# The first mixer of a two-layer hybrid decoder: four conv tiles by Silu, the q products of both token tiles together, and three sets of order edges for the state-space decays

## The chip, the cores and the metric

The kernel runs on one core of a Trainium2 chip. The metric is device microseconds of one execution of the whole program. Before the change the median of three runs is 1026.51 us (1025.82 to 1027.15).

The engines are named as in the profile: PE is TensorE (PEld its weight loads), DVE is VectorE, ACT is ScalarE, POOL is GpSimd, SP is SyncE.

## The reference, cut to what matters

Two layers. Each is a feed-forward block, a mixer and a feed-forward block, all added to the residual x (256 tokens by 1024, float32). The change touches only the mixer of the first layer, which joins a state-space part (SSD, 16 heads in 4 groups) and a latent attention part (MLA, 8 heads):

```python
xbc = silu(causal_depthwise_conv(h @ w_xbc, w, b))   # 2048 columns: x | B | C
dt  = softplus(dt_raw + bias);  a = dt * A           # A = -exp(a_log)
a_cs = cumsum(a)                                     # within a chunk of 128 tokens
CB   = C @ B.T                                       # per chunk and group
Lmat = exp(a_cs[l] - a_cs[s]) for s <= l, else 0     # "decays", per head
y_diag = (CB * Lmat) @ (x * dt)
y_off  = exp(a_cs) * (C @ state)
y = rms_norm((y_diag + y_off + d_skip * x) * silu(z))
q = rms_norm(q_a @ w_qb); k, v = from(kv_a @ w_kvb)  # rope on 32 of 96 columns
o = softmax(q @ k.T, causal) @ v
x = x + concat(y, o) @ w_out
```

The outputs must agree with this to float32-like accuracy, which is why each product is made of three.

## The kernel before, in words

**Weights.** Every weight matrix is loaded once, in pieces of at most 128 x 1024 float32 (512 KB), in the order in which the program uses them. `Stream.load` issues the load on SP's queue into `raw` (four buffers, L89), ACT casts it to `wh` (L93, eight buffers, float32r) and DVE writes what the cast lost into `wl` (L96, eight buffers). This DVE subtraction is called the *split* below. A `raw` buffer is free for the next load when its split is done. A product is three matmuls: hi x hi, hi x lo and lo x hi (L298 to L300 for products by token, L315 to L317 by channel, L345 to L347 for the output projection).

**Tokens and banks.** The 256 tokens are two tiles of 128, t = 0 and 1. PSUM has four banks for products (`bank`, names `p_...`), and two plus two for small ones (`sbank`, names `m_...`). A product that takes a bank waits for the last reader of the product that held it.

**The order of the work.** The program is written in one order, and a scheduler with a timeline simulation then lays out the instruction order of each engine. It may move an instruction past others that are ready later by its estimate. `self.order(later, earlier)` adds an edge to it: in the laid out order `later` may not stand ahead of `earlier`. On the chip every engine works through its own list in order, and waits on semaphores where an operand or a buffer comes from another engine.

**The first mixer** (some 196 to 376 us of the profiled execution) is written so:

1. `xbc(8)` to `xbc(11)`: the four column tiles of B. `xbc(c, out)` loads one tile of weights, makes the product with 24 matmuls of 256 columns, and `conv_silu` makes the convolution: one ACT instruction (L489) and three of DVE (L491). Silu is then made of `Tanh` on ACT (L494) and one more DVE instruction (L495).
2. The q products `p_qb`, for t = 0 and then t = 1: two halves each, of nine matmuls of 384 columns. ACT reads each half three times (square L575, and the copies `qnat` L577 and `qr` L578). After the two halves of a tile come its rope, its norm factor, its eight transposes `m_qT` and the copies of them (L588).
3. `xbc(12)`, the kv products `p_kvb` of t = 0, `xbc(13)`, those of t = 1. ACT reads each p_kvb three times (square L606, `V` L608, `knat` L609); the transposes `m_kT` are copied with a gain to `kT` (L620).
4. softplus and the decay sums: `dte` by Abs and Exp (L421, L424; the Exp needs a table load), a polynomial on DVE (L428), `dts` L626, `a` L630, the cumulative sum `m_acs` on PE (L633), its transpose, and a write to DRAM by POOL (`acs_rows`, L642). Each row is later read back, spread over all partitions.
5. `xbc(14)` and `xbc(15)`, then the scores and softmax of both tiles and the products with V (`m_att_o`).
6. `decays(t)`: `m_CB` (L694), its masked copy `cb` (L696, DVE), two loads `E` (L700, POOL's queue, 512 KB each), sixteen Relu (L706) and four Exp (L709) on ACT, and four products with cb on DVE (L712). Only the first Relu of a tile is ordered behind the softmax.
7. `xbc(0)` to `xbc(7)` and their transposes `m_xsT`, then `scan(0)` (`m_yd`, L746), `decays(1)`, and the four products `p_z` with their gates (ACT Tanh L758, DVE L759). `p_z` holds all four product banks, so the first matmul of the output projection `p_acc` takes the bank that the first gate has read.
8. The norm of the gated y, the states, `scan(1)`, and the output projection `p_acc`.

The lines that the change touches are L88 to L97, L418 to L432, L484 to L495, L549 to L588, L624 to L647, L687 to L716 and L748.

Of the kernel before, what the change touches and what calls it, by code (L numbers as in the profile page):

```python
# [7 lines left out]
F32 = dt.float32  # L8
# [3 lines left out]
AF = mybir.ActivationFunctionType  # L12
ALU = mybir.AluOpType
X = mybir.AxisListType.X

P = 128
# [34 lines left out]
ROW = {}  # L51
# [21 lines left out]
class Stream:  # L73
# [4 lines left out]
    def __init__(self, nc, pool, flat, raw_bufs, bufs):  # L78
        self.nc, self.pool, self.flat = nc, pool, flat
        self.raw_bufs, self.bufs = raw_bufs, bufs  # L80
        self.off = 0
        self.n = 0

    def load(self, widths):
        nc = self.nc
        res = []
        for i, x in enumerate(widths):
            raw = self.pool.tile([P, x], F32, tag="raw", name=f"raw{self.n}_{i}", bufs=self.raw_bufs)  # L88
            nc.sync.dma_start(out=raw, in_=self.flat[self.off:self.off + P * x].rearrange("(p w) -> p w", w=x))  # L89
            self.off += P * x  # L90
            hi = self.pool.tile([P, x], F32R, tag="wh", name=f"wh{self.n}_{i}", bufs=self.bufs)
            lo = self.pool.tile([P, x], F32R, tag="wl", name=f"wl{self.n}_{i}", bufs=self.bufs)
            self.cast = nc.scalar.copy(out=hi, in_=raw)  # L93
            if i == 0:
                self.first = self.cast
            nc.vector.tensor_tensor(out=lo, in0=raw, in1=hi.bitcast(F32), op=ALU.subtract)  # L96
            res.append((hi, lo))  # L97
        self.n += 1
        return res


class Net:
# [380 lines left out]

    def conv_silu(self, c, b, out):  # L484

        nc = self.nc
        cw = self.conv[:, c, :]
        v = self.small([P, S], "cv", bufs=3)
        nc.scalar.activation(out=v, in_=b, func=AF.Identity, scale=cw[:, 3:4], bias=cw[:, 4:5])  # L489
        for s in (1, 2, 3):  # L490
            nc.vector.scalar_tensor_tensor(out=v[:, s:], in0=b[:, :S - s], scalar=cw[:, 3 - s:4 - s], in1=v[:, s:],  # L491
                                           op0=ALU.mult, op1=ALU.add)
        th = self.small([P, S], "cth", bufs=2)
        self.tanh = nc.scalar.activation(out=th, in_=v, func=AF.Tanh)  # L494
        return nc.vector.scalar_tensor_tensor(out=out, in0=th, scalar=1.0, in1=v, op0=ALU.add, op1=ALU.mult)  # L495
# [12 lines left out]
    def mixer0(self, hT, x, after):  # L508
# [39 lines left out]

        def xbc(c, out):  # L549
            w = st.load([D])[0]  # L550
            b = self.bank([P, S], "xbc")
            self.in_ch(b, hT, w)
            return self.conv_silu(c, b, out)
        for i in range(4):
# [7 lines left out]
        kT = [self.blk([96, 8, P], f"kT{t}", grp="a") for t in range(2)]  # L562
        sq = self.small([P, 2, 8], "sqs")
        for t in range(2):
            qn = self.blk([P, 8, 96], "qnat", grp="a")
            qr = self.blk([P, 8, 2, 16], "qr")
            for j in range(2):
# [9 lines left out]
                nc.scalar.copy(out=qn[:, hs, :64], in_=b[:, :, :64])  # L577
                nc.scalar.copy(out=qr[:, hs, :, :], in_=b[:, :, 64:].rearrange("p a (s d) -> p a s d", s=2))  # L578
            roped = self.apply_rope(qn[:, :, 64:].rearrange("p a (s d) -> p a s d", s=2), qr, t, "q", 8)

# [10 lines left out]
        for t in range(2):  # L591
# [24 lines left out]
            for j in range(2):  # L616
                tp = self.tbank([96, 4, P], "kT", "a")
                for i in range(4):
# [4 lines left out]
        e = self.small([P, 2, 16], "dte")  # L623
        l1 = self.log1p_exp(dtv, e, "dtl", squares)  # L624
        dts = self.edge.tile([P, 2, 16], F32, tag="dts", name="dts", bufs=1)
        nc.vector.scalar_tensor_tensor(out=dts, in0=dtv, scalar=0.0, in1=l1, op0=ALU.max, op1=ALU.add)  # L626
        ea = self.small([P, 16], "ea")
        nc.scalar.activation(out=ea, in_=row[:, ROW["a_log"]], func=AF.Exp)
        a = self.small([P, 32], "a")
        nc.vector.scalar_tensor_tensor(out=a.rearrange("p (t h) -> p t h", t=2), in0=dts, scalar=-1.0,  # L630
                                       in1=ea.unsqueeze(1).broadcast_to([P, 2, 16]), op0=ALU.mult, op1=ALU.mult)
# [14 lines left out]
        for i in (2, 3):  # L646
            xbc(12 + i, BC[1][:, i, :])  # L647

# [31 lines left out]
        exps = []  # L680
# [9 lines left out]
        def decays(t):  # L690
# [7 lines left out]
            for j in range(2):  # L698
                h = 16 * t + 8 * j
                nc.gpsimd.dma_start(out=E[j], in_=rows[h:h + 8, :].partition_broadcast(P))  # L700
            for g in range(4):
                eb = E[g // 2][:, 4 * (g % 2):4 * (g % 2) + 4, :]

                for i in range(4):
                    h = t * 16 + 4 * g + i
                    first = nc.scalar.activation(out=eb[:, i, :], in_=eb[:, i, :], func=AF.Relu, scale=-1.0, bias=acs[:, h:h + 1])  # L706
                    if g == i == 0:
                        self.order(first, exps[t])
                nc.scalar.activation(out=eb, in_=eb, func=AF.Exp, scale=-1.0)  # L709
# [4 lines left out]

        E0 = decays(0)

# [23 lines left out]
        def scan(t, E):  # L740
            for j in range(2):
# [5 lines left out]
                nc.vector.tensor_tensor(out=xs[t][:, s], in0=b.rearrange("p a b -> p (a b)"), in1=xs[t][:, s], op=ALU.add)  # L747
        scan(0, E0)  # L748
        E1 = decays(1)

# [482 lines left out]
```

## Time and profile before

| | before |
|---|---|
| median of three runs | 1026.51 us (1025.82 to 1027.15) |
| the profiled execution | 1026.63 us, its span 1024.9 us |
| PE busy | 1004.7 us (98%) |
| DVE, ACT, POOL busy | 680.5, 573.9, 72.1 us |
| granted PE clock | 0.9 or more of full speed in each of 40 slices |
| DMA | 181 GB/s mean over the span |

The span is that of the trace, from the first to the last instruction; the 1.7 us beside it belong to the execution but not to the trace. Matmuls are pipelined: a record of a 128 x 512 matmul lasts about 0.39 us though the next one starts 0.23 us after it. So the time between two starts is what a matmul costs in a row of them, and a wait of PE costs the idle time that the trace shows and a little more, since the pipeline runs empty ahead of it.

### The profile page before, as it was taken

What the parts mean: (1) busy time and instruction counts of PE and PEld (TensorE: products, weight loads), DVE (VectorE), ACT (ScalarE), POOL (GpSimd) and SP (SyncE); (2) the same over time, 40 slices, a digit from 0 to 9 for tenths busy, and PEclk for the clock granted to TensorE, in tenths of its full rate; (3) what the DMA queues carried; (4) which work ended last, traced back from release to release, by engine and by line L of the source; (5) the groups of instructions that cost most, each with busy time, mean ns of one, the idle gap of its engine ahead of it and who ended that gap; (6) DMA issues with size and microseconds to landing.
All of it is one profiled execution on the core that took longest, in us unless ns stands there. A gap on an engine that the chain in (4) does not pass through costs nothing.

```text
span 1024.9 us, 15128 instructions
## 1 busy us (share of the span) xinstructions
PE 1004.7 (98%) x5609; PEld 863.5 (84%) x5609; DVE 680.5 (66%) x1053; ACT 573.9 (56%) x1043; POOL 72.1 (7%) x108
## 2 busy tenths in 40 slices
PE   6999999999999999999999999999999999999998
PEld 5888888898988888888888888888887778888886
DVE  6787754588796767677546767754578676776641
ACT  5665543388866466655434665553386456555530
POOL 2100000016132200000000000000020000000000
PEclk9999999999999999999999999999999999999999
DMA  8775555455455257555564655555564256555451
GB/s 294 265 224 190 196 181 185 137 204 173 146 171 174 87 196 255 188 195 193 187 198 150 229 192 194 187 183 169 165 209 140 84 164 199 192 185 188 162 185 42
DMA packets 52090, 185.95 MB, mean 181 GB/s; under 512 B 5911, under 2 KB 5928, under 8 KB 52016
## 3 DMA queue, kind: packets, MB, share of 16 engines
q1 hardware_dynamic: 49248, 176.58, 52.0%
q0 software_dynamic: 2048, 6.83, 2.1%
q10 hardware_dynamic: 720, 1.57, 0.4%
q8 instruction: 44, 0.72, 0.3%
q14 instruction: 30, 0.25, 0.1%
HBM read 183.89 MB, written 1.06 MB: 180 GB/s over the span
## 4 chain that ended last, share of the span: by engine, by line
PE 93%; ACT 3%; DMA 2%; DVE 1%; issue 1%; POOL 1%; POOLq 0%; DVEq 0%; ACTq 0%
PE p_u L326 13%; PE p_g L326 13%; PE p_acc L346 9%; PE p_acc L345 9%; PE p_acc L347 9%; PE p_u L328 7%; PE p_g L328 7%; PE p_u L300 1%; PE p_u L298 1%; PE p_u L299 1%; PE p_g L298 1%; PE p_g L299 1%; PE p_g L300 1%; PE m_nrm L135 1%; PE p_xbc L315 1%; PE p_tok L298 1%
## 5 line engine op out<-in xcount | busy, mean ns | idle before, releaser
L96 DVE TENSOR_TENSOR wl<-raw,wh 128x1024 fp32r<-128x1024 f32 (+3 forms) x341 | 410.2, 1213 | 222.5 <-ACT wh L93 220.8
L93 ACT CAST wh<-raw 128x1024 fp32r<-128x1024 f32 (+3 forms) x341 | 352.3, 1040 | 298.3 <-PE p_acc L346 99.5
L326 PE MATMUL p_g<-hT,wh 128*128 128x512 f32 x576 | 203.2, 391 | 0.0
L326 PE MATMUL p_u<-hT,wh 128*128 128x512 f32 x576 | 203.1, 391 | 0.0
L328 PE MATMUL p_g<-hT,wl 128*128 128x256 f32 x576 | 161.6, 281 | 0.0
L328 PE MATMUL p_u<-hT,wl 128*128 128x256 f32 x576 | 161.3, 280 | 0.0
L347 PE MATMUL p_acc<-wl,acth 128*128 128x512 f32 x352 | 137.1, 389 | 0.0
L346 PE MATMUL p_acc<-wh,actl 128*128 128x512 f32 x352 | 137.0, 389 | 0.0
L345 PE MATMUL p_acc<-wh,acth 128*128 128x512 f32 x352 | 136.2, 391 | 0.0
L326 PEld LDWEIGHTS p_u<-hT,wh 128*128 128x128 f32 x576 | 107.7, 187 | 23.8
L326 PEld LDWEIGHTS p_g<-hT,wh 128*128 128x128 f32 x576 | 107.8, 187 | 23.6
L328 PEld LDWEIGHTS p_g<-hT,wl 128*128 128x128 f32 x576 | 108.8, 189 | 0.2
L328 PEld LDWEIGHTS p_u<-hT,wl 128*128 128x128 f32 x576 | 108.9, 189 | 0.0
L347 PEld LDWEIGHTS p_acc<-wl,acth 128*128 128x128 f32 x352 | 66.1, 188 | 13.8
L345 PEld LDWEIGHTS p_acc<-wh,acth 128*128 128x128 f32 x352 | 66.1, 188 | 13.6
L346 PEld LDWEIGHTS p_acc<-wh,actl 128*128 128x128 f32 x352 | 66.1, 188 | 13.4
L255 POOL TENSOR_TENSOR ss<-ss,mhalf 128x1 f32<-128x1 f32 x12 | 6.7, 558 | 578.7 <-DVE ss L273 578.7
L353 DVE SCALAR_TENSOR_TENSOR x<-p_acc,x 128x512 f32<-128x512 f32 x24 | 16.4, 688 | 39.4 <-PE p_acc L347 39.4
L315 PE MATMUL p_xbc<-hT,wh 128*128 128x256 f32 x128 | 36.8, 288 | 0.9 <-DVE cv L491 0.9
L317 PE MATMUL p_xbc<-hT,wl 128*128 128x256 f32 x128 | 36.6, 286 | 0.0
L316 PE MATMUL p_xbc<-hT,wh 128*128 128x256 f32 x128 | 36.2, 283 | 0.0
L409 DVE TENSOR_TENSOR sg<-sg 128x256 f32<-128x256 f32 x72 | 30.6, 425 | 7.8 <-DVE sg L406 0.9
(373 smaller groups left out, 1495.5 us busy)
## 6 DMA issues: line engine op xcount, KB each, us to landing
raw<-in_w SPq DMA_DIRECT2D x326, 512.0 KB, 4.3
gain<-in_gains POOLq DMA_DIRECT2D x5, 512.0 KB, 5.6
E<-acs_rows POOLq DMA_DIRECT2D x4, 512.0 KB, 6.1
raw<-in_w SPq DMA_DIRECT2D x4, 400.0 KB, 3.1
raw<-in_w SPq DMA_DIRECT2D x4, 288.0 KB, 2.8
raw<-in_w SPq DMA_DIRECT2D x3, 384.0 KB, 3.5
raw<-in_w SPq DMA_DIRECT2D x4, 272.0 KB, 2.9
out<-x ACTq DMA_DIRECT2D x4, 256.0 KB, 2.0
```

Source lines behind the costliest of these rows:

```text
L93: self.cast = nc.scalar.copy(out=hi, in_=raw)
L96: nc.vector.tensor_tensor(out=lo, in0=raw, in1=hi.bitcast(F32), op=ALU.subtract)
L298: mm(out, ah, wh, start=first and i == 0, stop=False)
L315: mm(out, hi[:, cs], xh, start=k == 0, stop=False)
L316: mm(out, hi[:, cs], xl, start=False, stop=False)
L317: mm(out, lo[:, cs], xh, start=False, stop=k == KT - 1)
L326: first = mm(out, hi[:, cs], hT[k // 2][:, k % 2], start=k == 0, stop=k == KT - 1, skip_group_check=True)
L328: second = mm(out[:, 0, :], lo[:, cs], self.hk(hT, k)[0], start=False, stop=k == KT - 1, skip_group_check=True)
L345: first = nc.tensor.matmul(o, ah, w[0][:, s], start=k == 0, stop=False)
L346: nc.tensor.matmul(o, al, w[0][:, s], start=False, stop=False)
L347: nc.tensor.matmul(o, ah, w[1][:, s], start=False, stop=k == nk - 1)
L409: nc.vector.tensor_tensor(out=sg, in0=sg, in1=v[:, 1, :], op=ALU.mult)
```

## The change

Line numbers of the changed kernel are about ten higher; instructions keep their names.

- `conv_silu` gets an argument `table`. For the tiles of B (8 to 11) it makes `Silu` of twice the convolution in one ACT instruction, and the DVE instruction L495 is not made.
- The q loop becomes two: first the products and reads of both token tiles, then rope, norm and transposes of both.
- `dte` (its Abs) and `ea` (an Exp of a parameter) are ordered behind the last of the four Silu.
- `Stream` keeps its casts and splits in lists, and `xbc(14)` and `xbc(15)` order their splits behind `a`, the last step of the decay sums on DVE.
- `decays` is cut in two. `decays` keeps CB, cb and the loads of E; `exponents` has the Relu, the Exp and the products with cb. It is written as `scan(0, exponents(0, ...))` after the x tiles, and every Relu is ordered behind the last Exp of the softmax of its tile.

```diff
+        self.casts, self.rests = [], []
...
-            nc.vector.tensor_tensor(out=lo, in0=raw, in1=hi.bitcast(F32), op=ALU.subtract)
+            self.casts.append(self.cast)
+            self.rests.append(nc.vector.tensor_tensor(out=lo, in0=raw, in1=hi.bitcast(F32), op=ALU.subtract))
...
-    def conv_silu(self, c, b, out):
+    def conv_silu(self, c, b, out, table):
...
+        if table:
+            self.silu = nc.scalar.activation(out=out, in_=v, func=AF.Silu, scale=2.0)
+            return self.silu
...
-        def xbc(c, out):
+        def xbc(c, out, behind=None):
             w = st.load([D])[0]
+            if behind is not None:
+                self.order(st.rests[-1], behind)
             b = self.bank([P, S], "xbc")
             self.in_ch(b, hT, w)
-            return self.conv_silu(c, b, out)
+            return self.conv_silu(c, b, out, 8 <= c < 12)
...
-        for t in range(2):
-            qn = self.blk([P, 8, 96], "qnat", grp="a")
-            qr = self.blk([P, 8, 2, 16], "qr")
+        qns = [self.blk([P, 8, 96], "qnat", grp="a") for _ in range(2)]
+        qrs = [self.blk([P, 8, 2, 16], "qr") for _ in range(2)]
+        for t in range(2):
+            qn, qr = qns[t], qrs[t]
...
+        for t in range(2):
+            qn, qr = qns[t], qrs[t]
             roped = self.apply_rope(qn[:, :, 64:].rearrange("p a (s d) -> p a s d", s=2), qr, t, "q", 8)
...
-        l1 = self.log1p_exp(dtv, e, "dtl", squares)
+        l1 = self.log1p_exp(dtv, e, "dtl", self.silu)
...
-        nc.scalar.activation(out=ea, in_=row[:, ROW["a_log"]], func=AF.Exp)
+        self.order(nc.scalar.activation(out=ea, in_=row[:, ROW["a_log"]], func=AF.Exp), self.silu)
...
-            xbc(12 + i, BC[1][:, i, :])
+            xbc(12 + i, BC[1][:, i, :], last)
...
+            return E, cb
+
+        def exponents(t, E, cb):
             for g in range(4):
...
-                    if g == i == 0:
-                        self.order(first, exps[t])
+                    self.order(first, exps[t])
...
-        E0 = decays(0)
+        first_decays = decays(0)
...
-        scan(0, E0)
-        E1 = decays(1)
+        scan(0, exponents(0, *first_decays))
+        E1 = exponents(1, *decays(1))
```

Where the change moves instructions, three places of the laid out order follow. A row is the line, the operation, output<-input with the buffer's number, and the shape.

**DVE, at the end of the decay sums.** `wl` is a split: before, the one here is that of a later x tile, and those of `xbc(14)`, `xbc(15)` and `xbc(0)` stand further up. Before:

```order
L610 TENSOR_SCALAR rk_2407<-rk_2407,ssn_1913 128x8
L495 SCALAR_TENSOR_TENSOR CT_2063<-cth_2384,cv_2379 128x256
L428 SCALAR_TENSOR_TENSOR dtl_2541<-dtl_2541,dte_2538 128x32
L611 TENSOR_SCALAR rk_2407<-rk_2407 128x8
L428 SCALAR_TENSOR_TENSOR dtl_2541<-dtl_2541,dte_2538 128x32 x5
L626 SCALAR_TENSOR_TENSOR dts<-dtv_1911,dtl_2541 128x32
L96 TENSOR_TENSOR wl_0_2973<-raw_0_2970,wh_0_2972 128x1024
L630 SCALAR_TENSOR_TENSOR a_2556<-dts,ea_2554 128x32
```

Of the change:

```order
L430 SCALAR_TENSOR_TENSOR dtl_2533<-dtl_2533,dte_2530 128x32
L621 TENSOR_SCALAR rk_2399<-rk_2399,ssn_1913 128x8
L637 SCALAR_TENSOR_TENSOR dts<-dtv_1911,dtl_2533 128x32
L622 TENSOR_SCALAR rk_2399<-rk_2399 128x8
L641 SCALAR_TENSOR_TENSOR a_2548<-dts,ea_2546 128x32
L98 TENSOR_TENSOR wl_0_2567<-raw_0_2564,wh_0_2566 128x1024
L98 TENSOR_TENSOR wl_0_2606<-raw_0_2603,wh_0_2605 128x1024
L98 TENSOR_TENSOR wl_0_2820<-raw_0_2817,wh_0_2819 128x1024
L98 TENSOR_TENSOR wl_0_2859<-raw_0_2856,wh_0_2858 128x1024
```

No split stands ahead of `a` any more, and the splits of `xbc(14)` (2567), `xbc(15)` (2606), `xbc(0)` (2820) and `xbc(1)` (2859) stand in a row behind it, with all four `raw` buffers.

**ACT, around the reads of the last kv products.** `knat_2488`, of the change `knat_2480`, is made from the two kv products of t = 1 (`p_kvb_2497` and `p_kvb_2509`; of the change `p_kvb_2489` and `p_kvb_2501`). In the changed program the matmuls of `xbc(15)` take the bank of the first of the two and wait for its last reader. Before they took the bank of `xbc(13)`. Before:

```order
L93 CAST wh_0_3028<-raw_0_3026 128x1024
L644 ACTIVATE eacs_2570<-acs_2560 128x16
L93 CAST wh_0_3067<-raw_0_3065 128x1024
L606 ACTIVATE junk_2516<-p_kvb_2509 128x256
L608 COPY V_2238<-p_kvb_2509 128x256
L494 ACTIVATE cth_2485<-cv_2480 128x256
L640 COPY acsT_2564<-m_acsT_2562 32x128
L620 ACTIVATE kT_172_2241<-m_kT_2437,kgain_156 96x512
L609 COPY knat_2488<-p_kvb_2497 128x4x64
L609 COPY knat_2488<-p_kvb_2509 128x4x64
```

Of the change:

```order
L94 CAST wh_0_2897<-raw_0_2895 128x1024
L94 CAST wh_0_2936<-raw_0_2934 128x1024
L655 ACTIVATE eacs_2562<-acs_2552 128x16
L617 ACTIVATE junk_2508<-p_kvb_2501 128x256
L619 COPY V_2230<-p_kvb_2501 128x256
L94 CAST wh_0_2992<-raw_0_2990 128x1024
L492 ACTIVATE cv_2595<-p_xbc_2570,conv_145 128x256
L631 ACTIVATE kT_168_2233<-m_kT_2429,kgain_156 96x512
L620 COPY knat_2480<-p_kvb_2489 128x4x64
L620 COPY knat_2480<-p_kvb_2501 128x4x64
```

`knat` now stands behind the casts of `xbc(2)`, `xbc(3)` and `xbc(4)` (2897, 2936, 2992) and behind the convolution of `xbc(14)`.

**PE, at the end of the z products.** Before, the tail of the attention and `m_CB` of t = 1 stand so, and the last 24 matmuls of `p_z` (`p_z_3385`, all of them) begin behind them:

```order
L457 MATMUL m_att_o_2789<-pT_257_2763,V_2238 64x128 x2
L694 MATMUL m_CB_3218<-CT_2063,BT_2062 128x128 x4
L299 MATMUL p_z_3357<-wh_1_3353,hT_42_228 128x512
L300 MATMUL p_z_3357<-wl_1_3354,hT_42_228 128x512
L457 MATMUL m_att_o_2789<-pT_260_2776,V_2238 64x128 x2
L457 MATMUL m_att_o_2789<-pT_257_2763,V_2238 64x128 x2
L457 MATMUL m_att_o_2789<-pT_260_2776,V_2238 64x128 x2
L298 MATMUL p_z_3385<-wh_0_3335,hT_39_225 128x512
```

Of the change:

```order
L459 MATMUL m_att_o_2781<-pT_253_2755,V_2230 64x128 x2
L705 MATMUL m_CB_3210<-CT_2063,BT_2062 128x128 x4
L137 MATMUL m_Bn_3442<-sq,BT_2062 128x128 x4
L459 MATMUL m_att_o_2781<-pT_256_2768,V_2230 64x128 x2
L459 MATMUL m_att_o_2781<-pT_253_2755,V_2230 64x128 x2
L459 MATMUL m_att_o_2781<-pT_256_2768,V_2230 64x128 x2
L347 MATMUL p_acc_3527<-wh_0_3533,oT_232_2644 128x512
```

All of `p_z` now stands ahead of the scan, the attention's tail and `m_CB`, and only `m_Bn` and three pairs of `m_att_o` are left between `m_CB` and the output projection. On DVE the order there is `cb`, the four products of E and then the gates, where before three gates stood ahead of the last product of E. On ACT the last copy to `pT` (from `m_pT_2775`), which the three pairs of `m_att_o` behind `m_Bn` wait for, stands behind the sixteen Relu and the first two Exp of E, and the first gate's Tanh behind all four Exp. The first of the two loads of E waits for the sixth matmul of the last 24 of `p_z`, whose weights lay where it lands.

## Rows read from the trace of the kernel before

**Rows 1.** Waits of PE by line and releaser, 196 to 376 us (the first mixer).

```profile
PE p_qb L298 <- ACT qr L578: 1.0, 1, 1.0
PE p_xbc L315 <- DVE cv L491: 0.9, 1, 0.9
PE p_kvb L298 <- ACT qr L578: 0.7, 1, 0.7
PE m_acs L633 <- DVE a L630: 0.5, 1, 0.5
PE p_acc L345 <- ACT yT L250: 0.4, 1, 0.4
```

**Rows 2.** Timeline of PE at 238 us: start, length, instruction, count, idle before.

```profile
238.07 1.03 PE L135 MATMUL m_qT<-sq,qnat 128*96 128x128 f32 x8
239.78 0.50 PE L298 MATMUL p_kvb<-wh,kvT 128*128 128x512 f32 x1 [0.67 <-ACT qr L578]
```

**Rows 3.** Timeline of DVE at 245 us, the end of the decay sums.

```profile
244.65 0.19 DVE L626 SCALAR_TENSOR_TENSOR dts<-dtv,dtl 128x32 f32<-128x32 f32 x1
245.32 1.23 DVE L96 TENSOR_TENSOR wl<-raw,wh 128x1024 fp32r<-128x1024 f32 x1 [0.48 <-ACT wh L93]
246.46 0.60 DVE L630 SCALAR_TENSOR_TENSOR a<-dts,ea 128x32 f32<-128x32 f32 x1
```

**Rows 4.** Transfers to the tile raw, 225 to 260 us: time from issue to landing.

```profile
DMA to landing us min/median/max: 3.2/4.3/7.7
```

**Rows 5.** Timeline of ACT at 252 us.

```profile
252.21 0.63 ACT L609 COPY knat<-p_kvb 128x256 f32<-128x256 f32 x2
252.73 0.70 ACT L620 ACTIVATE kT<-m_kT,kgain 96x512 f32<-96x512 f32 x1
253.31 1.05 ACT L93 CAST wh<-raw 128x1024 fp32r<-128x1024 f32 x1
254.25 0.58 ACT L489 ACTIVATE cv<-p_xbc,conv 128x256 f32<-128x256 f32 x1
```

**Rows 6.** Timeline of PE at 251 us, at the end of `xbc(14)`.

```profile
252.57 0.28 PE L317 MATMUL p_xbc<-hT,wl 128*128 128x256 f32 x1
```

**Rows 7.** Timeline of PE, 309 to 323 us.

```profile
309.56 2.12 PE L746 MATMUL m_yd<-xd,E 128*128 128x64 f32 x18
...
313.25 1.31 PE L457 MATMUL m_att_o<-pT,V 128*64 128x128 f32 x20
314.50 1.16 PE L694 MATMUL m_CB<-CT,BT 128*128 128x128 f32 x8
...
316.05 0.88 PE L457 MATMUL m_att_o<-pT,V 128*64 128x128 f32 x12
316.86 0.50 PE L298 MATMUL p_z<-wh,hT 128*128 128x512 f32 x1
...
322.46 0.60 PE L135 MATMUL m_Bn<-sq,BT 128*128 128x128 f32 x4
```

**Rows 8.** Timeline of DVE, 315 to 321 us.

```profile
315.69 0.69 DVE L696 TENSOR_TENSOR cb<-m_CB,sq 128x512 f32<-128x512 f32 x1 [3.22 <-PE m_CB L694]
316.48 1.90 DVE L712 TENSOR_TENSOR E<-E,cb 128x512 f32<-128x512 f32 x3
...
318.29 1.88 DVE L759 SCALAR_TENSOR_TENSOR gate<-gate,p_z 128x512 f32<-128x512 f32 x3
```

**Rows 9.** Transfers to the tile E in the whole program: time from issue to landing.

```profile
DMA to landing us min/median/max: 4.0/6.1/7.0
```

**Rows 10.** Timeline of ACT, 307 to 320 us.

```profile
307.36 2.45 ACT L706 ACTIVATE E<-E,acs 128x128 f32<-128x128 f32 x8 [1.73 <-DMA E<-acs_rows]
309.71 1.14 ACT L709 ACTIVATE E<-E 128x512 f32<-128x512 f32 x2
...
317.44 1.54 ACT L758 ACTIVATE gate<-p_z 128x512 f32<-128x512 f32 x3
```

**Rows 11.** Two stretches at the program's start: us, busy us by engine, granted PE clock, DMA.

```profile
0.00:9.50 9.50, 0.00 (x0) 0.00 (x0) 0.96 (x3) 4.06 (x7) 2.32 (x12) 1.00 0.78 283
9.50:12.00 2.50, 2.44 (x10) 2.18 (x11) 2.14 (x4) 1.29 (x3) 0.00 (x0) 1.00 1.02 419
```

More of the change, by code (lines that the diff above doesn't have):

```diff
@@ L492, in conv_silu @@
                                            op0=ALU.mult, op1=ALU.add)
+        if table:
+            self.silu = nc.scalar.activation(out=out, in_=v, func=AF.Silu, scale=2.0)
+            return self.silu
         th = self.small([P, S], "cth", bufs=2)
-        self.tanh = nc.scalar.activation(out=th, in_=v, func=AF.Tanh)
+        nc.scalar.activation(out=th, in_=v, func=AF.Tanh)
         return nc.vector.scalar_tensor_tensor(out=out, in0=th, scalar=1.0, in1=v, op0=ALU.add, op1=ALU.mult)
@@ L627, in mixer0 @@
         ea = self.small([P, 16], "ea")
-        nc.scalar.activation(out=ea, in_=row[:, ROW["a_log"]], func=AF.Exp)
+        self.order(nc.scalar.activation(out=ea, in_=row[:, ROW["a_log"]], func=AF.Exp), self.silu)
         a = self.small([P, 32], "a")
-        nc.vector.scalar_tensor_tensor(out=a.rearrange("p (t h) -> p t h", t=2), in0=dts, scalar=-1.0,
+        last = nc.vector.scalar_tensor_tensor(out=a.rearrange("p (t h) -> p t h", t=2), in0=dts, scalar=-1.0,
                                        in1=ea.unsqueeze(1).broadcast_to([P, 2, 16]), op0=ALU.mult, op1=ALU.mult)
```

## The prediction, made before the changed kernel ran

> **What bounds the kernel now.** I read the share of busy time first, then the waits of PE in the stretch of the first mixer, then the timelines of PE, ACT and DVE around each wait, and last the laid out order of the changed program beside them. PE is busy nearly all of the span, so the time of this kernel is PE's work plus its waits. The change takes no matmul away. What it can give back is therefore bounded by the waits of PE in this stretch: 1.0 + 0.9 + 0.7 + 0.5 + 0.4 = 3.5 us of idle time [rows 1]. A wait costs a little more than its idle time: between the starts of the eight `m_qT` and of the `p_kvb` behind them lie 1.71 us, of which the eight need about 0.8 (1.03 less the 0.25 in which the last one runs out), so 0.9 us are lost for an idle time of 0.67 [rows 2]. I add 0.25 us to each wait. On the other side there is no such bound: DVE and ACT have free time, and what they do later than before shows only where PE, or a buffer, comes to wait for it. A measurement of this kernel can tell about 0.2% (2.05 us) from no change.
>
> **The change part by part.**
>
> *Silu in one instruction.* Four instructions of DVE (L495) go, ACT keeps its count, and the number of table loads stays the same; one of them moves from ahead of the Exp of `dte` to behind the last read of q. PE never waits for the tiles of B here, so this is worth nothing by itself: the cover is the q, kv and C products, which all come before the first `m_CB`.
>
> *q products together.* The wait of `p_qb`, 1.0 us [rows 1], stays: the second half of a tile still takes the bank whose last reader is the copy `qr` of the first. On ACT a convolution now stands ahead of that read and a Tanh no longer behind it; I charge 0.1 us (0 to 0.5, one convolution of 0.58 us [rows 5]). The wait of `p_kvb` goes: ACT made the `qr` copy of t = 1 only behind a copy of the transposed q of t = 0, and now reads all q products first. Gain 0.7 + 0.25 = 0.95 us.
>
> *Decay sums ahead of a split.* The wait of `m_acs` for `a` goes. Before, `dts` was done at 244.84 but `a` stood behind a split that itself waited 0.48 us for its cast and took 1.23 us [rows 3]; three more splits had delayed the polynomial. In the new order none stands ahead of it. The polynomial then follows the sums of squares of the second kv product, which I follow to `a` done at 243.0 (0.5 either way). Gain 0.5 + 0.25 = 0.75 us.
>
> The price of this: the splits of `xbc(14)`, `xbc(15)`, `xbc(0)` and `xbc(1)` stand behind `a`, and with them all four `raw` buffers. Before, the loads of `xbc(2)` to `xbc(5)` had gone out well ahead of `a`. Now they go as the splits end, at 1.15 us each: 244.2, 245.3, 246.5 and 247.6. A transfer to `raw` takes 3.2 to 7.7 us here, 4.3 in the median [rows 4], so the tiles land at about 248.5, 249.6, 250.8 and 252. Behind these landings stands ACT's queue: the casts of `xbc(2)` and `xbc(3)`, three short instructions (0.9 us), the cast of `xbc(4)`, the convolution of `xbc(14)`, one `kT` copy, and then the `knat` copy that gives back the bank which the matmuls of `xbc(15)` need. The cast of `xbc(3)` ends at 250.6, that of `xbc(4)` begins at 251.5 and takes 0.94, the convolution 0.5, `kT` 0.6, `knat` 0.3 [rows 5]: the bank is free at 253.9. PE reached the end of `xbc(14)` at 252.69, 0.12 after the start of its last matmul [rows 6], and comes 0.95 + 0.75 - 0.1 = 1.6 us earlier, at 251.1. **New wait: 2.8 us.** The ends: with loads at 3.2 us it is 1.7, with `a` half a microsecond later 3.3; and if the loads were no hindrance at all, only the `kT` copy and `knat` would be late, 0.5 us. I take the median load, since these four come in a row, as most loads of that view do.
>
> The Trainium skill ("DMA: Bandwidth & Descriptors", section "Anatomy of one DMA — SWDGE (gpsimd) path") gives a transfer a fixed part of 2.0 us and its bytes at 436 GB/s, an estimate of 3.2 us for 512 KB. The view agrees with that as its smallest value only, 3.2 against a median of 4.3 [rows 4]; by the page the new wait would be 1.7 us, the sum 1.1 us lower, and the forecast 1028.3.
>
> *Relu behind softmax.* The wait of the last x tile, `p_xbc` for the convolution of an earlier one, 0.9 us [rows 1], goes: DVE's products with cb no longer stand ahead of it. Gain 0.9 + 0.25 = 1.15 us. The scores, `m_xsT` and `p_z` keep a margin of 2 us or more as I follow them, so I cost the later Relu of t = 0 at nothing; its cover is the whole of `p_z`, since the scan now comes behind it.
>
> *The end of p_z.* Here the laid out order changes most. Before, from the start of `m_CB` at 314.50 to `p_acc`, PE had two pairs of things to do: twelve `m_att_o` and 24 matmuls of `p_z`, 316.86 to 322.46, 5.6 us [rows 7]. In that time DVE made cb, the products of E and the gates [rows 8]. Now the 24 stand ahead. Let T be the end of the sixth of them, when the first load of E can go. PE then has six transposes (0.6), 18 matmuls at 0.23 (4.1), eight transposes (0.8), 32 `m_yd` at 0.107 (3.4; 18 took 2.12 with 0.2 of running out), four transposes (0.4), 20 `m_att_o` (1.25) and `m_CB` (1.0) [rows 7]: it starts `m_CB` at T + 10.5, `m_Bn` at T + 11.5, the last `m_att_o` at T + 11.9, and would start `p_acc` at T + 12.7.
>
> `p_acc` needs the bank that the first gate reads. On DVE: cb 1.19 after the start of `m_CB`, then 0.79, four products of 0.6, and the gate of 0.68 [rows 8]: T + 11.7, 12.5, 14.9, 15.6. On ACT: E lands 4.0 to 7.0 us after its issue, 6.1 in the median [rows 9], so at T + 6.2; eight Relu 2.45, a cast 0.95, eight Relu 2.45, two Exp 1.1 [rows 5, 10]: T + 13.1; then the copy to `pT` (0.5), for which the last `m_att_o` wait: T + 13.7; two more Exp, T + 14.7; the Tanh (0.5), T + 15.2. The last product of E ends then at about T + 15.4, the gate at T + 16.1. **New wait: 3.4 us**, some 1.8 of it at `m_att_o` for ACT and 1.6 at `p_acc` for DVE. With E landing in 4.0 us DVE's own chain holds, T + 15.6, 2.9 us; with 7.0 us it is 4.3.
>
> *The end of the mixer.* Four matmuls of `p_acc` now stand between the two `m_yT`, which covers the wait for the copy `yT`: gain 0.4 + 0.25 = 0.65 us (0 to 0.9).
>
> **The sum.** Gone: 0.95 + 0.75 + 1.15 + 0.65 = 3.5. New: 0.1 + 2.8 + 3.4 = 6.3. Together +2.8 us on the profiled execution's 1026.63, whose span is 1024.9, so 1029.4. The median of the three runs is 0.12 us lower, so the forecast is **1029.3 us**, slower by 0.27%. Its own range, with all ends of the two new waits: 1.7 + 2.9 to 3.3 + 4.3, so +1.2 to +4.2, 1027.7 to 1030.7.
>
> **The rivals.**
>
> *A. The loads are no hindrance (not slower).* The place is the `knat` copy on ACT. If `a` is done by about 240, or the loads land in under 2 us, the cast of `xbc(4)` is over before the `kT` copy can run, and the wait is 0.5 us in place of 2.8: **1027.0 us**, no difference that can be told. For it: DVE has four splits less to do ahead of `a`, and my time for `a` rests on following some thirty instructions. Against it: no transfer in the view took less than 3.2 us [rows 4]. Chance 0.17.
>
> *B. The end of p_z costs nothing.* If the gates were made before the products of E, or the bank were free for another reason, `p_acc` would start at T + 12.7: **1025.9 us**, also no difference. Against it stand both laid out orders, ACT's and DVE's. Chance 0.08. *A and B together* give **1023.6 us**, faster by 0.28%: chance 0.09.
>
> *C. The gains don't come.* The waits that go are replaced by others of their size, because DVE with its late splits holds up the convolutions or the row sums of the softmax between 255 and 300 us: +6.3, up to **1032.8 us**. For it: DVE gets some 5 us of splits later than before. Against it: by 260 us it had caught up in my replay. Chance 0.08.
>
> *D. The clock.* PE stands still for about 3 us twice. In the trace it stood still for the first 9.5 us and had a granted clock of 1.00, the 2.4 GHz level, in that stretch and in the one behind it [rows 11], so the trace speaks against any loss. If the clock fell to 1.2 GHz after one of the new waits and stayed there for as long as the wait, 3.4 us, the work of that stretch would lose half of it, 1.7 us: **1031.0 us**. Chance 0.04. The Trainium skill ("TensorE: Matmul & The Clock Gate", section "What's actually happening") has the array fall to 1.2 GHz when it has been idle for long enough, and by that rule a fall would be possible here; the trace does not show one [rows 11].
>
> **How the numbers follow.** The forecast's own case has 0.54, A 0.17, B 0.08, both 0.09, C 0.08, D 0.04. Faster by over 0.2% (below 1024.5) is A with B, and a small rest: 0.10. Within 0.2% are A, B and the lower end of the own range up to 1028.6 (0.10): 0.35. Slower are the rest of the own range, C and D: 0.55. For a range that holds 8 in 10 I leave out A with B at the bottom and C at the top: from 1025.9 to 1031.0 us.
>
> **What would show it.** In the waits of PE in the first mixer: no `m_acs` for `a`, no `p_kvb` for `qr`, none of an x tile for a convolution; `p_qb` for `qr` still about 1.0; new `p_xbc` for ACT `knat` about 2.8, `m_att_o` for ACT `pT` about 1.8 and `p_acc` for DVE `gate` about 1.6. On SP the loads of `xbc(2)` to `xbc(5)` go out after `a`. The forecast is wrong if `p_xbc` doesn't wait for `knat` (A), if `p_acc` starts right behind `m_att_o` (B), if PE waits for DVE between 255 and 300 us (C), or if a granted clock under 1 follows a wait (D).

## The result, and the profile of the changed kernel

| | before | changed |
|---|---|---|
| median (runs) | 1026.34 us (4) | **1035.05 us** (4; 1033.57 to 1036.3) |
| ratio, 95% interval | | 1.0080, 1.0069 to 1.0092 |
| the profiled execution, its span | 1026.63, 1024.9 us | 1034.57, 1032.8 us |
| PE busy, PE idle | 1004.7, 20.2 us | 1007.5, 25.3 us |

The change makes the kernel slower by 0.8%. The forecast was 1029.3 us and the range ended at 1031.0: the sign was right, and the size was a third of what came. Executions of one kernel differ by 1.3 to 4.6 us here, so times are compared by medians, and traces by their own spans.

The span grew by 7.9 us, in two parts: PE stands idle 5.1 us longer, and it is busy 2.8 us longer with the same 5609 matmul records. The waits of PE in the first mixer, 196 to 386 us of the changed kernel (engine, line and releaser: us in total, times, longest):

```profile
PE p_xbc L317 <- ACT knat L620: 3.7, 1, 3.7
PE p_acc L347 <- DVE gate L772: 2.6, 1, 2.6
PE p_qb L300 <- ACT qr L587: 1.2, 1, 1.2
PE m_att_o L459 <- DVE pT L480: 0.7, 1, 0.7
PE m_yd L759 <- DVE xd L749: 0.6, 1, 0.6
```

Against [rows 1], the four waits that were to go are gone: `p_kvb`, `m_acs`, `p_xbc` for a convolution, `p_acc` for `yT`, 2.5 us together. The two new ones that were forecast are there, and two small ones beside them. That makes the longer idle time: 3.7 + 2.6 + 0.7 + 0.6 + 0.2 (at `p_qb`) - 2.5 = 5.3.

The longer busy time lies right behind the two large waits. The timeline of PE in the changed kernel (start, length, instruction, idle time before), at the start of `xbc(15)` and of the output projection:

```profile
255.15 0.39 PE L317 MATMUL p_xbc<-hT,wh 128*128 128x256 f32 x1 [3.67 <-ACT knat L620]
255.38 0.38 PE L318 MATMUL p_xbc<-hT,wh 128*128 128x256 f32 x1
255.55 0.42 PE L319 MATMUL p_xbc<-hT,wl 128*128 128x256 f32 x1
255.77 0.42 PE L317 MATMUL p_xbc<-hT,wh 128*128 128x256 f32 x1
...
258.91 0.28 PE L317 MATMUL p_xbc<-hT,wh 128*128 128x256 f32 x1
259.03 0.28 PE L318 MATMUL p_xbc<-hT,wh 128*128 128x256 f32 x1
...
329.95 0.50 PE L347 MATMUL p_acc<-wh,oT 128*128 128x512 f32 x1 [2.58 <-DVE gate L772]
...
330.94 0.63 PE L347 MATMUL p_acc<-wh,oT 128*128 128x512 f32 x1
331.37 0.63 PE L348 MATMUL p_acc<-wh,oT 128*128 128x512 f32 x1
...
334.16 0.40 PE L349 MATMUL p_acc<-wl,oT 128*128 128x512 f32 x1
334.39 0.39 PE L347 MATMUL p_acc<-wh,oT 128*128 128x512 f32 x1
```

Read the starts, not the lengths. Fifteen matmuls of 256 columns, from 255.55 on, start 0.213 us apart, and from 258.76 on 0.12 apart. Eight of 512 columns, from 330.52 on, start 0.427 apart, and then 0.23. So 15 x 0.093 = 1.4 us and 8 x 0.195 = 1.6 us are lost, 3.0 together, for the 2.8 of longer busy time. Two stretches of the changed kernel (us; busy us of PE, its weight loads, DVE, ACT, POOL; granted PE clock, DMA):

```profile
255.50:258.50 3.00, 3.00 (x16) 3.00 (x15) 2.00 (x5) 2.77 (x5) 2.11 (x2) 0.50 0.84 298
330.50:333.50 3.00, 3.00 (x8) 2.32 (x7) 3.00 (x6) 1.05 (x5) 0.00 (x0) 0.50 0.00 0
```

The granted clock is 0.50, the 1.2 GHz level. The same two stretches of the kernel before, with 27 and 15 matmuls in them for 16 and 8:

```profile
255.50:258.50 3.00, 3.00 (x27) 3.00 (x27) 3.00 (x7) 1.51 (x2) 1.72 (x3) 1.00 0.69 228
330.50:333.50 3.00, 3.00 (x15) 2.55 (x14) 0.00 (x0) 1.40 (x3) 0.00 (x0) 1.00 0.76 239
```

The page with its 40 slices is too coarse for this: it says 0.9 or more in every slice for both kernels. The Trainium skill ("TensorE: Matmul & The Clock Gate", section "What's actually happening") has the array fall to 1.2 GHz after idling, and this trace agrees: 0.50 right behind waits of 3.67 and 2.58 us.

**Why `xbc(15)` waits for `knat`.** DVE and ACT of the changed kernel, 243 to 255 us:

```profile
243.74 0.19 DVE L641 SCALAR_TENSOR_TENSOR a<-dts,ea 128x32 f32<-128x32 f32 x1
243.85 5.05 DVE L98 TENSOR_TENSOR wl<-raw,wh 128x1024 fp32r<-128x1024 f32 x4
...
248.39 1.06 ACT L94 CAST wh<-raw 128x1024 fp32r<-128x1024 f32 x1 [1.47 <-DMA raw<-in_w]
250.52 1.05 ACT L94 CAST wh<-raw 128x1024 fp32r<-128x1024 f32 x1 [1.08 <-DMA raw<-in_w]
...
252.76 1.04 ACT L94 CAST wh<-raw 128x1024 fp32r<-128x1024 f32 x1 [0.54 <-DMA raw<-in_w]
253.71 0.56 ACT L492 ACTIVATE cv<-p_xbc,conv 128x256 f32<-128x256 f32 x1
254.17 0.67 ACT L631 ACTIVATE kT<-m_kT,kgain 96x512 f32<-96x512 f32 x1
254.74 0.63 ACT L620 COPY knat<-p_kvb 128x256 f32<-128x256 f32 x2
```

`a` starts 2.7 us earlier than in [rows 3]. The four splits run in a row behind it and give the `raw` buffers back one by one; the next loads land late, some 2.1 to 2.2 us apart, ACT stands idle for them three times (1.47, 1.08, 0.54 us), and `knat` stands behind the three casts.

**Why `p_acc` waits for the gate.** DVE of the changed kernel at the end of the mixer:

```profile
326.01 0.69 DVE L707 TENSOR_TENSOR cb<-m_CB,sq 128x512 f32<-128x512 f32 x1 [0.16 <-PE m_CB L705]
326.80 2.50 DVE L725 TENSOR_TENSOR E<-E,cb 128x512 f32<-128x512 f32 x4
329.21 1.88 DVE L772 SCALAR_TENSOR_TENSOR gate<-gate,p_z 128x512 f32<-128x512 f32 x3
```

In [rows 8] this chain lay beside 24 matmuls of `p_z` [rows 7]. Now they stand ahead of `m_CB`, and PE has twelve `m_att_o` left beside it.

### The profile page after: what moved, and what is told of

It is laid out like the page before. It is cut to its first block, busy times and chain, and to the rows that moved or that the text cites. A ratio compares the mean times of both kernels' runs of the same rounds, so it can differ in the third digit from the quotient of the medians.

```text
span 1032.8 us, 15128 instructions
## 1 busy us (share of the span) xinstructions
PE 1007.5 (98%) x5609; PEld 866.3 (84%) x5609; DVE 682.9 (66%) x1049; ACT 574.3 (56%) x1043; POOL 73.2 (7%) x108
## 4 chain that ended last, share of the span: by engine, by line
PE 91%; DVE 3%; ACT 3%; DMA 2%; issue 1%; POOL 0%; DVEq 0%; ACTq 0%; SPq 0%; POOLq 0%
PE p_g L328 13%; PE p_u L328 13%; PE p_acc L348 9%; PE p_acc L349 9%; PE p_acc L347 9%; PE p_u L330 7%; PE p_g L330 7%; PE p_u L302 1%; DMA raw<-in_w 1%; PE p_u L300 1%; PE p_u L301 1%; PE p_g L300 1%; PE p_g L301 1%; PE p_g L302 1%; DVE wl L98 1%
```

## The experiments

The theory: two new waits of PE, each followed by a stretch at 1.2 GHz, make the loss. The edges on the splits cause the first, those on every Relu the second. The rivals: waits for the loads themselves, the late place of the Relu, or a loss that comes with the other two parts. All ratios are to the kernel before, whose medians beside these runs were 1026.80 to 1026.98 us.

### Taking parts back

*Without the edges on the splits:*

```diff
-            xbc(12 + i, BC[1][:, i, :], last)
+            xbc(12 + i, BC[1][:, i, :])
```

> The change, without the two order edges that put the splits of xbc(14) and xbc(15) behind a. Theory (two new waits of PE, each followed by a stretch at the lower clock): the wait of xbc(15) for knat, 3.7 us, goes, and with it the stretch at half the granted clock behind it, 1.7 us; the wait of m_acs for a comes back, 0.75 us; the waits at the end of p_z stay, with their low stretch. So some 4.9 us less than the change, 1030.1 us, and one window with a granted clock near 0.83 in place of two. Rival 1 (the late splits alone make DVE late up to the end of p_z): both waits go, about 1025 us. Rival 2 (the Silu and q parts cost the time): 1033 us or more.

Measured: 1028.70 us, ratio 1.0012 (1.0003 to 1.0021), 1.4 us under the forecast. The wait for `knat` is gone. No wait of `m_acs` for `a` came back, so the other parts had already removed it, and the edges bought nothing. The second wait stayed and kept its low clock (the waits, then the stretch):

```profile
PE p_acc L347 <- DVE gate L772: 2.4, 1, 2.4
```

```profile
320.00:330.00 10.00, 7.65 (x48) 5.88 (x45) 8.32 (x14) 7.63 (x20) 2.34 (x4) 0.83 0.25 81
```

*With the exponents back at the place of their loads, and only the first Relu of a tile ordered:*

```diff
-                    self.order(first, exps[t])
+                    if g == i == 0:
+                        self.order(first, exps[t])
...
-        first_decays = decays(0)
+        E0 = exponents(0, *decays(0))
...
-        scan(0, exponents(0, *first_decays))
+        scan(0, E0)
```

> The change, with decays as before: the exponents of t = 0 written at the place of the loads, and only the first Relu of a tile ordered behind the softmax. Theory: the last matmuls of p_z stand behind m_CB again, so the waits at m_yd, m_att_o and p_acc (0.6 + 0.7 + 2.6 us) go and the low stretch behind them (1.7 us) too; the wait of xbc(15) for knat, 3.7 us, and its low stretch stay; an x tile may wait for a convolution again, 1.1 us. So 4.5 to 5.6 us less than the change, 1029.4 to 1030.5 us. Rival 1 (the late splits are the one cause): 1034 to 1035 us, with p_acc still waiting for a gate.

Measured: 1033.24, ratio 1.0063 (1.0048 to 1.0078), slower than expected. The wait for the gate is gone, that for `knat` is still 3.8 us, and in the newly laid out order another of the same kind stands where none was (the wait, then the stretch):

```profile
PE m_sc L674 <- ACT kT L631: 2.3, 1, 2.3
```

```profile
270.00:280.00 10.00, 7.65 (x51) 7.46 (x51) 5.70 (x12) 10.00 (x27) 0.96 (x2) 0.83 0.21 78
```

*Both edits, so that Silu and the q products remain:*

> Silu and the q products together alone: neither the edges on the splits nor the cut in decays. Theory: no wait above 1.2 us in the first mixer, granted clock 1.00 throughout; the wait of p_kvb for qr (0.95 us) gone against the kernel before: 1025.4 us, faster than before by 0.1%. Rival 2 (Silu or the q order cost part of the 8.7 us): 1028 us or more.

Measured: 1029.65, ratio 1.0024 (1.0015 to 1.0034): a miss, and the rival's time. Both waits are gone, but `m_sc` waits 2.1 us for DVE's `oT` (clock 0.83 from 290 to 300 us) and `m_CB` 1.3 us for `CT`.

*No edges on the splits, only the first Relu ordered, but the late place kept:*

> The change without the edges on the splits, and with only the first Relu of a tile ordered behind the softmax; the exponents stay where the change writes them. Theory: neither of the two waits, and the wait of an x tile for a convolution (1.1 us) gone as in the change: 1024.3 us, 0.2% under the kernel before. Rival: the place where the exponents are written, not the edges on the other Relu, moves p_z ahead of m_CB; then p_acc waits for a gate again, about 1030 us.

Measured: 1028.48, ratio 1.0016 (1.0006 to 1.0026): a miss in time. No wait for the gate, although the exponents stand late, and most of the last 24 matmuls of `p_z` stand behind `m_CB` again: the late place alone does not bring all of `p_z` ahead of it, the edges on all sixteen Relu have to be there too. Whether these edges would do it with the exponents in their old place was not tried. `m_sc` for `oT` costs 1.5 us and `m_CB` for `CT` 1.1; the clock stays at 1.00.

*The kernel before with one part of the change alone, the q products together (first diff), then Silu (second):*

```diff
         for t in range(2):
...
+        for t in range(2):
+            qn, qr = qns[t], qrs[t]
             roped = self.apply_rope(qn[:, :, 64:].rearrange("p a (s d) -> p a s d", s=2), qr, t, "q", 8)
```

```diff
+        if table:
+            self.silu = nc.scalar.activation(out=out, in_=v, func=AF.Silu, scale=2.0)
+            return self.silu
...
```

The second kernel also orders `dte` and `ea` behind the last Silu, as the change does.

> The kernel before with the q products of both tiles together alone. Theory (a part pays by the waits its laid out order leaves, not by its own work): the wait of p_kvb for qr goes, 0.95 us, and if no wait of 2 us or more comes in, 1025.9 us. Rival (the q order itself brings the waits seen with Silu and q, m_sc for oT and m_CB for CT): 1029 to 1030 us.

> The kernel before with Silu for the tiles of B alone, and its edges on dte and ea. Theory (Silu's own work costs PE nothing; only a wait that the new laid out order brings in would show): 1026 to 1027 us if no wait of 2 us or more comes in; if one does, 1029 us or more and a window with a granted clock under 0.9. Rival (the table load behind the q reads delays ACT and PE waits for it): a wait of p_kvb or m_qT for ACT of over 1 us.

Measured: 1033.06, ratio 1.0060 (1.0045 to 1.0075), and 1035.36, ratio 1.0078 (1.0061 to 1.0096). Both were expected to change little. With the q products alone `m_sc` waits 2.4 us for `kT` and 1.6 for `oT`, and the clock is 0.66 from 270 to 280 us; with Silu alone `m_pT` waits 5.8 us for a softmax product that POOL makes late, behind a reciprocal on DVE that ends at 281.0, and it is 0.66 from 280 to 290. Two of the waits with Silu alone:

```profile
PE m_pT L135 <- POOL p L465: 5.8, 1, 5.8
PE p_kvb L298 <- ACT qr L581: 1.8, 1, 1.8
```

The second is the sign that the rival named. It was 0.7 us before [rows 1]. The table load, 1.28 us on ACT, stood at 219.3 us before and stands at 235.9 here, ahead of the last reads of q. Some 1.1 us of the 8 lie at that wait; whether the load or the rest of the new order made it, no run tells. So the parts' costs can't be added: a small edit makes the scheduler lay out another order, and that order has waits of its own.

### One edge at each wait

*The last 24 matmuls of `p_z` ordered behind the last `m_CB` of t = 1 (`first_mm` is the first of the 24):*

```diff
+                if t and j:
+                    self.order(self.first_mm, self.cb_mm)
```

> The change with one more order edge: the first of the last 24 matmuls of p_z behind the last m_CB of t = 1. PE's order is that of the change up to the end of the third p_z. Theory: the wait of xbc(15) for knat, 3.7 us, and the low stretch behind it, 1.7 us, stay as they are; the waits at m_yd, m_att_o and p_acc (3.9 us) and the low stretch behind them (1.7 us) go, since 24 matmuls cover the gates: 5.6 us less than the change, 1029.5 us. Rival (work between 260 and 310 us costs part of the 8.7 us): 1032 us or more.

Measured: 1030.64, ratio 1.0037 (1.0025 to 1.0050), 1.1 us over the forecast: the wait for the gate and its low clock are gone and that for `knat` (3.1 us, clock 0.85 from 250 to 260) stays, as expected, but `m_yd` still waits 0.9 us.

*The casts of `xbc(2)` to `xbc(4)` ordered behind the last `knat`:*

```diff
+            if c in (2, 3, 4):
+                self.order(st.casts[-1], self.knat)
```

> The change with three more order edges: the casts of xbc(2), xbc(3) and xbc(4) behind the last knat copy. The splits stay behind a, so the loads go out as late as in the change. Theory (ACT's casts, which wait for those loads, hold up knat): the wait of xbc(15) falls from 3.7 to 0.8 us or less and no low stretch follows: 4.6 us less. PE's order after it also leaves 15 matmuls of p_z between m_CB and p_acc, 3.4 us of cover, so the wait there falls under 1 us without a low stretch: 4.6 us less again, 1025.9 us in all. Rival 1 (the late loads themselves bound PE, which then waits for the weights of xbc(2) or xbc(3)): a new wait of an x tile for a cast or split of 2 to 3 us, about 1030 us.

Measured: 1028.24, ratio 1.0018 (1.0008 to 1.0028), 2.3 us over the forecast. The wait for `knat` is gone and no x tile waits for its weights, so the casts' place in ACT's queue made the wait, and not the late loads by themselves. The new order happens to have no wait for the gate, but `p_z` waits 2.9 us for a convolution, with the clock at 0.93 and 0.90 in the two stretches behind it.

*Both edges:*

> The change with the edges of both, those on the casts and the one on p_z. Theory: neither wait, granted clock 1.00 in the whole mixer: 1025 us, under the kernel before by about 1 us. Rival (the waits come out elsewhere, as in the kernel with Silu and q alone): 1028 us or more, with a wait of m_sc, m_CB or an x tile of over 1 us.

Measured: 1029.52, ratio 1.0028 (1.0017 to 1.0039): a miss, and the rival's case. Both waits are gone, but that of `p_z` for a convolution, 2.9 us, is here too.

### The clock by itself

The changed kernel with useless transposes in front of the waits: PE then has something to do while it waits for ACT or DVE. First the transpose of the decay sums made 30 times; then also the four of `m_Bn` seven times.

```diff
-        self.transpose(bt, acs)
+        for _ in range(30):
+            self.transpose(bt, acs)
...
-        for g in range(4):
+        for g in list(range(4)) * 7:
```

> The change, with the transpose of the decay sums (m_acsT) made 30 times in place of once; the 29 more write the same values. They stand on PE where it waits for knat, so PE works through most of that wait. Theory (PE's standing still brings its clock down): the matmuls of xbc(15) start when they did, at about 255.1 us, but at a granted clock of 1.00, so 1.7 us less than the change, 1033.3 us, and the wait for knat in the profile shrinks to under 1 us. The wait for the gate and its low stretch stay. Rival (the slow matmuls behind the wait are slowed by the casts and loads around them, or every wait has a price of its own): 1035 us and a window at 0.83 in 255 to 265.

> As the one with 30 transposes of the decay sums, and the four transposes m_Bn made seven times, with the same values, on PE where it waits for the gate. Theory: no low stretch behind either wait: 3.3 us less than the change, 1031.7 us, granted clock 1.00 through the mixer, though PE's own work grew by 53 transposes. Rival: as the change, 1035 us.

Measured: 1032.22, ratio 1.0048 (1.0032 to 1.0063), and 1029.94, ratio 1.0027 (1.0016 to 1.0037). That is 2.8 and 5.1 us less than the changed kernel, with 29 and 53 matmuls more. PE of the first of the two:

```profile
251.03 3.44 PE L137 MATMUL m_acsT<-sq,acs 128*32 128x128 f32 x30
...
255.51 0.39 PE L317 MATMUL p_xbc<-hT,wh 128*128 128x256 f32 x1 [0.82 <-ACT knat L620]
255.73 0.28 PE L318 MATMUL p_xbc<-hT,wh 128*128 128x256 f32 x1
255.85 0.27 PE L319 MATMUL p_xbc<-hT,wl 128*128 128x256 f32 x1
```

`xbc(15)` starts no earlier than in the changed kernel (255.51 against 255.15), but its matmuls are 0.12 us apart from the second on. The stretch behind each wait, of the first (only the first wait filled), then of the second (both filled):

```profile
255.00:265.00 10.00, 9.49 (x80) 9.50 (x81) 9.04 (x16) 7.38 (x14) 5.26 (x5) 1.00 0.82 257
320.00:330.00 10.00, 7.36 (x50) 6.10 (x49) 9.17 (x15) 8.43 (x23) 1.39 (x3) 0.84 0.26 94
```

```profile
255.00:265.00 10.00, 9.41 (x79) 9.22 (x79) 9.13 (x15) 7.37 (x15) 5.21 (x5) 1.00 0.81 256
320.00:330.00 10.00, 10.00 (x83) 8.91 (x82) 9.12 (x14) 8.42 (x23) 1.68 (x2) 1.00 0.29 107
```

Each stretch is at 1.00 where its wait was filled, and only there. At the gate the two kernels are alike but for the 24 transposes: DVE works in the same order, and from the first `m_CB` to the first `p_acc` it is 6.11 us in the first and 6.10 in the second. Only the clock behind differs. So standing idle, and not the wait as such, brings the 1.2 GHz level.

The totals say less. More came back than the 1.4 and 1.6 us counted above, but the added matmuls also changed the laid out order: in both kernels the last twelve `m_att_o` stand behind the first `p_acc`, and `m_yd` no longer waits. The price of the clock is read from the stretches, not from these medians.

### Towards a better version

*Without the edges on the splits, and the last of `p_z` behind `m_CB`:*

> The change without the edges on the splits, and with the last 24 matmuls of p_z ordered behind the last m_CB of t = 1. Theory: no wait over 1.2 us and no low stretch: the kernel without the split edges (1028.7 us) less its wait for the gate (2.4), the 0.3 at m_att_o and the low stretch (1.7): 1024.4 us, under the kernel before by 0.2%. Rival (the waits come out elsewhere again): 1028 us or more.

Measured: median 1029.92, ratio 1.0016 (1.0001 to 1.0030), a miss. The ten times fall into two groups, four at 1026.57 to 1027.30 and six at 1029.86 to 1031.18; the profile is of one in the first group and shows no wait over 1.2 us. What the others do differently stays open.

*The two single edges, and the Relu of t = 0 ordered behind ACT's convolutions of all x tiles:*

```diff
+                    if t == 0:
+                        self.order(first, self.conv_act)
```

> The change with the edges of both (casts behind knat, last p_z behind m_CB) and one more: the Relu of t = 0 behind the convolutions of all x tiles on ACT. Theory (the 5 us of Relu on ACT hold up the convolution of an x tile, for which the first p_z waits 2.9 us in the kernel with both edges): that wait and the lower clock behind it go, some 4 us less than that kernel's 1029.5 us: 1025.5 us, and no wait over 1.7 us is left. Rival (DVE's splits hold up that convolution): the wait of p_z for DVE stays, 1029 us.

Measured: 1027.08, ratio 1.0005 (0.9996 to 1.0014), 1.6 us over the forecast: `m_st` now waits 1.4 us for ACT's `Bn`. The 2.9 us of `p_z` are gone: it was the Relu on ACT that had held up a convolution.

*The same edge, without the edges on the splits, and with the last of `p_z` behind `m_CB`:*

> The change without the edges on the splits, with the last p_z behind m_CB and the Relu of t = 0 behind the convolutions of all x tiles. Theory: no wait over 1.2 us, as in the kernel without the last edge (its profiled execution 1026.6 us), and less waiting at m_yd and m_pT: 1025.5 to 1026.5 us, no difference from the kernel before that can be told. Rival: 1029 us or more with a new wait.

Measured: **1025.19, ratio 0.9986 (0.9978 to 0.9995)**, faster than the changed kernel by 1.0%, and than the kernel before by 0.14%, which its interval only just tells from no change. Its page's line of busy times, and all its waits of PE in the first mixer:

```profile
PE 1004.5 (98%) x5609; PEld 863.3 (84%) x5609; DVE 679.3 (66%) x1049; ACT 573.4 (56%) x1043; POOL 72.3 (7%) x108
```

```profile
PE p_qb L300 <- ACT qr L589: 1.3, 1, 1.3
PE p_kvb L300 <- ACT knat L622: 0.2, 1, 0.2
PE p_kvb L300 <- DVE cv L496: 0.2, 1, 0.2
```

PE is busy as long as before the change, and idle for 1023.0 - 1004.5 = 18.5 us in place of 20.2: a gain of 1.7 us, of the 2.5 us of idle time that the prediction had counted as gone.

## Why the prediction was wrong

**What held.** All four waits went. `p_qb` waits 1.2 us (1.1 forecast). The mechanism at `knat` is the one that was followed, term by term: `a` at 243.9 (243.0), the cast of `xbc(4)` begun at 252.8 (251.5), the bank free at 255.15 (253.9), a wait of 3.7 us for 2.8. It is late by the 0.9 us of `a`, and by the loads: the sum gave each of the four the median of 4.3 us, but the casts that waited for them began at 248.39, 250.52 and 252.76, 2.1 and 2.2 us apart where the sum had the landings 1.1 to 1.2 apart.

The end of `p_z` cost 2.6 + 0.7 and, with `m_yd`, 0.6: 3.9 us for 3.4. That these sums lie so near each other is luck, since the parts differ. The loads of E landed in 4.3 and 5.0 us, not 6.1, so ACT's chain did not end last: the last `m_att_o` did not wait at all, and the wait for the gate was 2.6 us where 1.6 stood in the sum, near the 2.9 that the prediction gave to DVE's own chain. The 0.7 us is a wait of earlier `m_att_o`, ahead of `m_CB`, for a `pT` copy of DVE, and the 0.6 at `m_yd` stood in no term.

**What failed.** The step that failed is the clock: the sum has no term for it, and rival D, which has one, was put aside (chance 0.04) by this sentence: "In the trace it stood still for the first 9.5 us and had a granted clock of 1.00, the 2.4 GHz level, in that stretch and in the one behind it [rows 11], so the trace speaks against any loss." The column said so; the matmuls did not. Two views of the kernel before, the timeline of PE at its start and the window over it:

```profile
12.71 0.63 PE L298 MATMUL p_g<-wh,hT 128*128 128x512 f32 x1
13.14 0.63 PE L299 MATMUL p_g<-wh,hT 128*128 128x512 f32 x1
...
14.26 0.40 PE L299 MATMUL p_g<-wh,hT 128*128 128x512 f32 x1
14.49 0.40 PE L300 MATMUL p_g<-wl,hT 128*128 128x512 f32 x1
```

```profile
12.00:14.00 2.00, 2.00 (x6) 1.52 (x6) 1.94 (x4) 2.00 (x5) 0.00 (x0) 1.00 0.82 238
```

Matmuls of 512 columns started 0.43 us apart up to 14 us, and 0.23 apart behind: half speed after the one long idle stretch, under a column that says 1.00. The trace has no record of the granted clock before 14.05 us, and the column reads 1.00 where it has none. So the trace of before did show that PE is slow behind an idle stretch, but not whether 3 us of idle time are enough. The changed kernel showed that: 1.4 us lost behind one wait and 1.6 behind the other, where the sum had nothing. With 3.0 us more the forecast would have been 1032.3 us, still 2.7 short.

**The sum again**, on the profiled executions. Forecast +2.8, measured +7.9. Of the 5.1 between them, 2.8 are PE's longer busy time, in the main the clock: the 3.0 us at the two waits, less about 0.4 at the program's start, where the slow matmuls end at 13.1 us in the changed trace and at 14.0 in that of before (an estimate, half of the shorter slow time). PE's idle time grew by 5.1 us where the sum had 6.3 - 2.5 = 3.8: 1.3 more. The last 1.0 is the 0.25 us a wait that was credited to the four that went: as many came, and they take it back.

The slow start differs from one execution to the next: in the sixteen traces here PE begins at 9.4 to 9.7 us, and its matmuls come to full speed at 12.5 to 15.8. At half speed that is up to 1.6 us (an estimate from these times), a part of what executions of one kernel differ by.

**What else was read wrongly.** The gain of 0.75 us was put to the edges on the splits; without them the wait of `m_acs` did not return, so they brought the largest loss and nothing on the other side. Silu was "worth nothing by itself"; alone it cost 0.78%, by the order that was laid out around it and perhaps by its table load, which stood ahead of the reads of q. In the changed kernel, too, the table load does not stand behind the last read of q but ahead of it (234.0 us, the last `qr` at 239.0); there no wait of PE came of it. The title of the section of the Trainium skill that the prediction cites for a transfer's time names the path of GpSimd, and these loads go out on SP's queue; the forecast beside it should read 1028.2.

## What to carry to other kernels

Price a wait of a busy PE at its length plus the slow stretch behind it. The profiles here show a granted clock under 1.00 behind each of the twelve longest waits in the first mixer (2.1 to 5.8 us), and 1.00 behind the shorter ones; in the two cases that were counted it cost 1.4 and 1.6 us more. No run varied the length of a wait by itself, so no limit follows from this. Look at the distance between the starts of matmuls, and not at the clock column, where PE has just been idle. And where a scheduler lays out the order, cost a small edit by the order of the whole, not by its own instructions.

## What the runs showed of the hardware beyond that

A split can be held until POOL has ended its TENSOR_TENSOR. DVE and POOL of the changed kernel:

```profile
314.23 3.77 DVE L98 TENSOR_TENSOR wl<-raw,wh 128x1024 fp32r<-128x1024 f32 x1 [0.70 <-PE p_z L301]
317.92 1.27 DVE L749 TENSOR_TENSOR xd<-m_xsT,dts 128x512 f32<-128x512 f32 x2
320.85 2.07 DVE L98 TENSOR_TENSOR wl<-raw,wh 128x1024 fp32r<-128x1024 f32 x1
```

```profile
313.86 1.05 POOL L467 TENSOR_TENSOR p<-p,rden 128x512 f32<-128x512 f32 x1
314.87 2.04 POOL L750 TENSOR_TENSOR xs<-xs,row 128x512 f32<-128x512 f32 x2
320.80 1.04 POOL L809 TENSOR_TENSOR xd<-xd,dec 128x512 f32<-128x512 f32 x1 [3.89 <-PE m_yd L759]
```

A split takes 1.21 us in the mean; these two end at 318.00 and 322.92, 1.09 and 1.08 us after POOL's work (316.91, 321.84), as if they did all theirs behind it. It does not always go so: a split at 294.01 ran its 1.21 us beside POOL's TENSOR_TENSOR, and POOL's two from 292.93 took 3.20 us together, where the two at 314.87 took 2.04. The first of the two held splits made `xd` late, for which `m_yd` waited 0.6 us. The Trainium skill ("SBUF — State Buffer", section "Who interferes with whom") says that a DVE instruction with two inputs in SBUF shares a read interface with a GpSimd instruction that reads SBUF, and that one of the two then blocks; these rows agree. No run here took POOL's work away to try it.
